# Norm factors and rotation of q and k moved to VectorE between the chunks of the delta rule, in a one-core decoder layer

## The chip, the cores and the metric

The kernel runs on one core of a Trainium2 chip. The metric is the device time of one execution in microseconds (us). The median of three executions before the change is 690.14 us.

## The reference, cut to what matters

One decoder layer over 512 positions of width 1024. A combined projection feeds two groups of heads: group A is a gated DeltaNet (a delta rule worked chunk by chunk, then a gated norm), group B is sliding-window attention over q and k that are first normalised per head and then rotated. The two outputs are joined, projected, gated and added to x. A mixture of experts (32 experts, two per position) follows. The change touches only the norm and rotation of q and k in group B:

```
q = rope(rms_norm(q.reshape(bsz, seq, SWA_Q_HEADS, HEAD_DIM), q_norm), positions)   # 8 heads of 64
k = rope(rms_norm(k.reshape(bsz, seq, SWA_KV_HEADS, HEAD_DIM), k_norm), positions)  # 2 heads of 64
# rope: x1, x2 = halves of a head; out = [x1*cos - x2*sin, x1*sin + x2*cos]
state = state * exp(g_last) + k_dec^T v_new     # delta rule: one step per chunk
```

## The kernel before, in words

The 512 positions lie as four blocks (`tb`, `n`) of 128 rows on the partitions. The mixer is written as five generators (`delta_rule`, `ropes`, `products`, `modulations`, `out_gdn`); `weave` (L56) hands their pieces over in the order of the numbers they yield. The framework then builds one queue per engine at compile time: a piece handed over earlier goes first where both could run, and a later one may go ahead where its inputs and buffers are there and the engine would be idle. On the chip each of the queues of VectorE, ScalarE and GpSimd runs in the order so built. `later(r, after)` (L252) adds an edge that orders two instructions in the same queue without a semaphore.

What stands around the change:

- `chunk(n)` (L706), key 67: the delta rule's step for 128 rows. TensorE forms products with the state (L713, L719), VectorE corrects X (L715, L716) and scales (L721), TensorE forms `p_vn` (L724) and `p_u` (L730), VectorE updates the state `Sbd` in two halves (L735, L736; a copy, L738, in chunk 0), TensorE forms the output `p_o` (L741), which L744 adds up. `join64` and `join32` (L665, L689) run between the chunks, with copies on VectorE (L685, L700).
- `products()` (L1110): the weight projections on TensorE. The last four (keys 67 to 92, `p_proj` at L263 to L265) give z; each is taken out of PSUM by ScalarE (L786, L787) and finished by VectorE (L788). At 92.5 comes `rope_turn(tb)` (L866): TensorE turns the rotated q and k (L872, L879), ScalarE writes them to `qrT` and `kg` (L873, L880). From 99 on comes `attend(tb, kv)` (L885): scores (L894, L898), maxima on VectorE (L901), exponentials on ScalarE, and so on.
- `ropes()` (L1166): `head_scale` (L838) squares on ScalarE and sums per head on VectorE (L845 for q, L846 for k), key 87.9; `rsqrt_n` (L182) makes the norm factors with 12 small VectorE instructions; `rope(tb)` (L848), key 92.2, multiplies and rotates. For q (128x512 per block) one product (L855) and six half-size instructions (L859 to L864, 128x256) run on VectorE; for k (128x128) the same seven (128x128 and 128x64) run on GpSimd.
- `out_gdn()` (L1193): `router_operands` (16 products `p_cst`, L1036), `gate_rows` (L980, products L986) for the gate g1, and the scaling of the output weights `wo` by g1 on VectorE (L1002), their split (L269, L270), and the output projection `p_wo`.
- Temporary tiles `hsq`, `rp`, `tz`, the angle tiles `ang` and `sin_w` and the attention's `pT` share one pool of three buffers, "w2" (`fill_tile`, L388).

After the mixer come the second half of the output projection, the routing, and the experts, whose weights (3 MB each) stream in from HBM as buffers come free.

Of the kernel before, what the change touches and what calls it, by code (L numbers as in the profile page):

```python
# [14 lines left out]
ALU = mybir.AluOpType  # L15
AX = mybir.AxisListType
# [3 lines left out]
P = 128  # L20
# [4 lines left out]
NH = 8  # L25
HD = 64
# [43 lines left out]
def hybrid_layer(ctx, tc, x, c, positions, w_ada, b_ada, norm_mix, w_in, conv_w, a_log, dt_bias,  # L70
# [4 lines left out]
    x = x[0]  # L75
# [3 lines left out]
    out = out[0]  # L79

    V, A, G, T = nc.vector, nc.scalar, nc.gpsimd, nc.tensor
# [14 lines left out]
    def psg(shape, name, dt=F32):  # L96
        return psG.tile(shape, dt, tag="psg", name=name)
# [18 lines left out]
    def sm(name, shape=(P, NT, NH), dt=F32):  # L116
        return small.tile(list(shape), dt, name=name)
# [19 lines left out]
    EN = {'V': V, 'G': G}  # L137
# [44 lines left out]
    def rsqrt_n(y, ss, scale, extra=None):  # L182

        t = mw.tile([P, NT * (NH + 2)], F32, tag="nt", name="newton_t")
        n = 1
        for d_ in y.shape[1:]:
            n *= d_
        t = t[:, :n]
        if len(y.shape) == 3:
            t = t.rearrange("p (a b) -> p a b", a=y.shape[1])  # L190
        V.tensor_scalar(ss, ss, scale, EPS, op0=ALU.mult, op1=ALU.add)
        yi = y.bitcast(I32)
        V.tensor_scalar(yi, ss.bitcast(I32), 1, None, op0=ALU.arith_shift_right)
        V.tensor_scalar(yi, yi, -1.0, float(0x5F3759DF), op0=ALU.mult, op1=ALU.add)
        for i in range(3):
            V.tensor_tensor(out=t, in0=ss, in1=y, op=ALU.mult)
            V.scalar_tensor_tensor(t, t, -0.5, y, op0=ALU.mult, op1=ALU.mult)
            V.scalar_tensor_tensor(y, t, 1.5, y, op0=ALU.add, op1=ALU.mult)
        if extra is not None:
            V.tensor_scalar(y, y, extra, None, op0=ALU.mult)  # L200
# [11 lines left out]
    def rms_rstd(src, name):  # L212

        sq = work.tile([P, D], F32, tag="w4", name=f"sq_{name}")
        st = work.tile([P, 1], F32, tag="st", name=f"st_{name}", bufs=4)
        A.activation(sq, src, AF.Square, accum_out=st)
        last_pow[0] = rsqrt_(st, st, 1.0 / D)
        return st
# [27 lines left out]
    for tb in range(NT):  # L246
        xx = xts[tb // 2][:, tb % 2]
        r = rms_rstd(xx, f"x{tb}")
# [3 lines left out]
    def later(r, after=None):  # L252

        tc.add_manual_dep(r.ins, after or hold, NOSYNC)
        return r
# [49 lines left out]
    for kb in range(KB):  # L305
# [17 lines left out]
        for b in range(4):  # L323
            n = slice(b * P, (b + 1) * P)
# [53 lines left out]
    for n in range(1, 4):  # L378
        for i in range(2):
            o = 32 * n + 8 * i  # L380
# [4 lines left out]
    def chain_tile(name, shape=(P, 512)):  # L385
        return mw.tile(list(shape), F32, tag="c2", name=name, bufs=3)

    def fill_tile(name, shape=(P, 512)):  # L388
        return mw.tile(list(shape), F32, tag="w2", name=name, bufs=3)
# [37 lines left out]
    def row_heads(t):  # L427
        return t.rearrange("p (h d) -> p h d", d=HD)

    def bc_n(t, n):  # L430
        return t[:, n, :, None].to_broadcast([P, NH, HD])
# [5 lines left out]
    eglP = sm("eglP", (P, NT, 4))  # L437
# [61 lines left out]
    big = {}  # L499
# [149 lines left out]
    def TT(m):  # L649
        return big[f"TT{m // 16}"][:, m % 16]  # L650
# [50 lines left out]


    Sbd = sm("Sbd", (P, 4, P))
    G.memset(Sbd, 0.0)

    def chunk(n):  # L706
        t = slice(n * P, (n + 1) * P)
        qT, knT, knat = big["qT"], big["knT"], big["knat"]
        X = big["vb"][:, n]
        if n:  # L710
            pk = psg([P, 512], f"p_ks{n}")
            for b in range(4):
                T.matmul(pk[:, b * P:(b + 1) * P], knT[:, b, t], Sbd[:, b], start=True, stop=True)  # L713
            ks = chain_tile(f"ks{n}")
            V.tensor_tensor(out=row_heads(ks), in0=row_heads(pk), in1=bc_n(bG, n), op=ALU.mult)  # L715
            V.tensor_tensor(out=X, in0=X, in1=ks, op=ALU.subtract)  # L716
            pq = psg([P, 512], f"p_qs{n}")
            for b in range(4):
                T.matmul(pq[:, b * P:(b + 1) * P], qT[:, b, t], Sbd[:, b], start=True, stop=True)  # L719
            qs = chain_tile(f"qs{n}")  # L720
            V.tensor_tensor(out=row_heads(qs), in0=row_heads(pq), in1=bc_n(eG, n), op=ALU.mult)  # L721
        pv = psg([P, 512], f"p_vn{n}")
        for h in range(NH):
            T.matmul(pv[:, h * HD:(h + 1) * HD], TT(n * NH + h), X[:, h * HD:(h + 1) * HD], start=True, stop=True)  # L724
        vn = chain_tile(f"vn{n}")
        A.activation(vn, pv, AF.Copy)
        if n < NT - 1:
            pu = psg([P, 4, P], f"p_u{n}")
            for b in range(4):
                T.matmul(pu[:, b], knat[:, n, b * P:(b + 1) * P], vn[:, b * P:(b + 1) * P], start=True, stop=True)  # L730
            for i in range(2):
                r = slice(64 * i, 64 * i + 64)
                sd = Sbd[r, :, r]
                if n:
                    V.tensor_tensor(out=sd, in0=sd, in1=eglP[r, n, :, None].to_broadcast([64, 4, HD]), op=ALU.mult)  # L735
                    V.tensor_tensor(out=sd, in0=sd, in1=pu[r, :, r], op=ALU.add)  # L736
                else:
                    V.tensor_copy(sd, pu[r, :, r])  # L738
        po = psg([P, 512], f"p_o{n}")
        for h in range(NH):  # L740
            T.matmul(po[:, h * HD:(h + 1) * HD], E[n][:, h], vn[:, h * HD:(h + 1) * HD],  # L741
                     start=True, stop=True)
        if n:
            V.tensor_tensor(out=X, in0=po, in1=qs, op=ALU.add)  # L744
        else:
            A.activation(X, po, AF.Copy)
# [91 lines left out]
    def head_scale(tb):  # L838

        q_, k_ = big["sq_n"][:, tb], big["skv"][:, tb, 0:P]  # L840
        sq = fill_tile(f"hsq{tb}")
        sk = mw.tile([P, P], F32, tag="hk", name=f"hsk{tb}", bufs=2)
        A.activation(sq, q_, AF.Square)
        A.activation(sk, k_, AF.Square)
        V.tensor_reduce(big["ssh"][:, tb, 0:NH], row_heads(sq), axis=AX.X, op=ALU.add)  # L845
        V.tensor_reduce(big["ssh"][:, tb, NH:], row_heads(sk), axis=AX.X, op=ALU.add)  # L846

    def rope(tb):  # L848

        rt, rs = big["rt"], big["rsh"]  # L850
        for src, nh, o, r0 in ((big["sq_n"][:, tb], NH, 0, 0), (big["skv"][:, tb, 0:P], 2, 4, NH)):
            s_ = row_heads(src)
            tmp = row_heads(fill_tile(f"rp{tb}{nh}")[:, :nh * HD])
            e_ = [EN[x] for x in 'VVVGGG'[3 * (nh == 2):]]
            EN['VG'[nh == 2]].tensor_tensor(  # L855
                out=s_, in0=s_, in1=rs[:, tb, r0:r0 + nh, None].to_broadcast([P, nh, HD]), op=ALU.mult)
            lo, hi, t_lo, t_hi = s_[:, :, :HH], s_[:, :, HH:], tmp[:, :, :HH], tmp[:, :, HH:]
            cl, sl, ch_, sh_ = (rt[:, o + i, tb, None, :].to_broadcast([P, nh, HH]) for i in (0, 1, 3, 2))
            e_[1].tensor_tensor(out=t_hi, in0=lo, in1=sh_, op=ALU.mult)  # L859
            e_[1].tensor_tensor(out=t_lo, in0=hi, in1=sl, op=ALU.mult)  # L860
            e_[0].tensor_tensor(out=lo, in0=lo, in1=cl, op=ALU.mult)
            e_[0].tensor_tensor(out=hi, in0=hi, in1=ch_, op=ALU.mult)
            e_[2].tensor_tensor(out=lo, in0=lo, in1=t_lo, op=ALU.subtract)
            e_[2].tensor_tensor(out=hi, in0=hi, in1=t_hi, op=ALU.add)  # L864

    def rope_turn(tb):  # L866

# [176 lines left out]
    def delta_rule():  # L1044
# [49 lines left out]
        for n in range(NT):  # L1094
            yield 67
            chunk(n)
            if n + 1 < NT:
                join64(n + 1)
            if n + 2 < NT:
                join32(n + 2)  # L1100
# [63 lines left out]
        slots.done("qrT", "sq_n", "sr")  # L1164

    def ropes():  # L1166
        yield 87.9
        big["ssh"], big["rsh"] = sm("ssh", (P, NT, NR)), sm("rsh", (P, NT, NR))
        for tb in range(NT):
            head_scale(tb)  # L1170
        rsqrt_n(big["rsh"], big["ssh"], 1.0 / HD)
        for tb in range(NT):
            yield 92.2 + 0. * tb
            rope(tb)

    def modulations():
        seq = [(r, kb) for r in (1, 2) for kb in range(KB)]
# [15 lines left out]
    def out_gdn():  # L1193
# [16 lines left out]
        slots.done("kg")  # L1210

    weave(delta_rule(), ropes(), products(), modulations(), out_gdn())
    sh2e, A2e, g2c = mod["sh2e"], mod["A2e"], mod["g2"]

# [262 lines left out]
    def at_lanes(lane8):  # L1477
        return V.tensor_tensor(out=so_t, in0=lane8[:, :, None].to_broadcast([P, 8, P]),
                               in1=laneb[:, None, :].to_broadcast([P, 8, P]), op=ALU.is_equal)
# [53 lines left out]
    after = at_lanes(l8).ins.name  # L1533
    keep_table(add_up(NS, "s", idle), 0, NS)
    for u in range(2):
# [20 lines left out]
                    in1=ident[0:NE, None, 0:NE].to_broadcast([NE, 2, NE]), op=ALU.mult)  # L1556
# [12 lines left out]
    ps, after = table(of_expert(sD, NSTAT, NE, "d"), NS, NU - NS, "d")  # L1569
# [209 lines left out]
    for k, u in enumerate(run):  # L1779
# [50 lines left out]
        if k >= NS and prepare:  # L1830
            V = Behind(nc.vector, g_.made)
            if next(prepare, 0) == 0:
                prepare = None
            V = nc.vector
# [56 lines left out]
```

## Time and profile before

| | us |
|---|---|
| median of three executions | 690.14 (689.63 to 705.21) |
| the profiled execution: its own time | 690.03 |
| the profiled execution: span, first to last instruction | 688.0 |
| TensorE busy in the span | 621.2 (90%) |
| VectorE / ScalarE / GpSimd busy | 387.2 / 243.7 / 182.2 |

The profiled execution's own time is 2.0 us longer than its span and 0.1 us below the median. Times in the rows below are us from the start of the span. PE is TensorE, PEld its weight loads, DVE VectorE, ACT ScalarE, POOL GpSimd. A timeline row has start, duration (for merged instructions from the first start to the last end), engine, line, operation, output and inputs, count, and in brackets the idle time before it and what ended it.

### The profile page before, as it was taken

The numbers are of one execution on the slowest core, as the hardware profiler recorded it, in microseconds if no ns is written. First come the engines' busy times: TensorE is split into PE (matmuls) and PEld (weight loads), VectorE is DVE, ScalarE is ACT, GpSimd is POOL, SyncE is SP. The second block draws the span as 40 slices with busy tenths as digits, with TensorE's granted clock in tenths as the row PEclk, the third lists the DMA queues.
The fourth block names the chain that finished last, engine by engine and source line by source line (L and its number), as shares of the span: only waits on it lengthen the run. The fifth ranks groups of instructions, "written<-read, shape, count | busy, mean of one in ns | idle before, by whom it ended". The sixth has DMA issues, their size and how long they took to land.

```text
span 688.0 us, 10766 instructions
## 1 busy us (share of the span) xinstructions
PE 621.2 (90%) x3907; PEld 378.7 (55%) x3908; DVE 387.2 (56%) x808; ACT 243.7 (35%) x546; POOL 182.2 (26%) x259
## 2 busy tenths in 40 slices
PE   6899799988888999988879998899999999999984
PEld 2576554646567978875447887334343334444521
DVE  3343986698999325688887348311342434444724
ACT  3235554232334442328772243413213232222200
POOL 2501315162263386063452002101001121111100
PEclk9799999997999999999989999999999999999998
DMA  8992374174310300251028849599999999999973
GB/s 256 293 318 65 122 279 164 62 250 162 123 61 23 102 2 12 90 216 62 1 64 302 335 156 354 203 399 416 412 414 403 411 410 406 408 408 410 408 296 123
DMA packets 62805, 161.78 MB, mean 235 GB/s; under 512 B 7175, under 2 KB 32931, under 8 KB 56608
## 3 DMA queue, kind: packets, MB, share of 16 engines
q1 hardware_dynamic: 57216, 148.52, 58.3%
q0 software_dynamic: 3952, 6.81, 2.9%
q10 hardware_dynamic: 1584, 5.77, 2.1%
q8 instruction: 31, 0.51, 0.3%
q14 instruction: 22, 0.18, 0.1%
HBM read 158.72 MB, written 8.39 MB: 243 GB/s over the span
## 4 chain that ended last, share of the span: by engine, by line
PE 45%; DMA 27%; DVE 20%; POOL 3%; issue 2%; ACT 2%; SPq 1%; POOLq 0%; ACTq 0%; DVEq 0%
DMA w_p<-in_w_up_dram 15%; DMA w_p<-in_w_down_dram 6%; PE p_gu L1600 5%; PE p_y L1636 3%; DMA w_p<-in_w_gate_dram 3%; DVE prod L643 3%; PE p_proj L265 3%; PE p_proj L263 3%; PE p_proj L264 3%; PE p_wo L264 2%; PE p_wo L265 2%; PE p_wo L263 2%; DVE cv L397 2%; DVE R L645 2%; PE p_ada L284 1%
## 5 line engine op out<-in xcount | busy, mean ns | idle before, releaser
L1600 PE MATMUL p_gu<-w_p,xT 128*32 128x512 f32 (+2 forms) x560 | 95.9, 594 | 0.0
L270 POOL TENSOR_TENSOR wH<-w,wH 128x512 fp32r<-128x512 f32 x36 | 52.4, 1472 | 125.9 <-ACT wH L269 112.8
L1600 PEld LDWEIGHTS p_gu<-w_p,xT 128*32 128x32 f32 (+2 forms) x560 | 32.0, 123 | 61.4 <-issue 55.8
L1519 POOL DMA_INDIRECT gb<-xn_d,ids x16 | 16.2, 1014 | 160.4 <-PE p_x L1587 146.4
L1636 PE MATMUL p_y<-w_p,hT 128*32 128x512 f32 (+2 forms) x280 | 51.3, 597 | 3.7 <-DVE hT L1624 2.6
L1609 DVE TENSOR_TENSOR hid<-hid,p_gu 128x256 f32<-128x256 f32 x16 | 6.7, 421 | 82.6 <-ACT hid L1608 82.6
L1608 ACT ACTIVATE hid<-p_gu 128x256 f32<-128x256 f32 x16 | 6.1, 384 | 126.8 <-PE p_gu L1600 126.8
L1593 ACT ACTIVATE xT<-p_x,sh2e,A2e 128x128 f32<-128x128 f32 x128 | 46.3, 467 | 12.1 <-PE p_x L1587 11.3
L1638 DVE SCALAR_TENSOR_TENSOR y<-p_y,wts,rsl 128x512 f32<-128x512 f32 x32 | 24.0, 749 | 41.5 <-PE p_y L1636 41.5
L265 PE MATMUL p_proj<-hH,wH 128*128 128x512 f32 x96 | 40.8, 425 | 0.0
L263 PE MATMUL p_proj<-hH,wH 128*128 128x512 f32 x96 | 40.5, 422 | 0.0
L264 PE MATMUL p_proj<-hL,wH 128*128 128x512 f32 x96 | 40.0, 417 | 0.0
L1656 PE MATMUL p_add<-yHL,to 128*128 128x512 f32 x128 | 35.5, 417 | 2.9 <-DVE xr L1661 1.9
L1656 PEld LDWEIGHTS p_add<-yHL,to 128*128 128x128 f32 x128 | 21.5, 188 | 19.7 <-DVE xr L1661 8.0
L1636 PEld LDWEIGHTS p_y<-w_p,hT 128*32 128x32 f32 (+2 forms) x280 | 14.8, 122 | 31.0 <-issue 24.4
L1661 DVE TENSOR_TENSOR xr<-xr,p_add 128x512 f32<-128x512 f32 x40 | 26.8, 686 | 6.9 <-PE p_add L1656 6.9
L263 PE MATMUL p_nat<-wH,hH 128*128 128x256 f32 x96 | 28.0, 291 | 0.0
L643 DVE TENSOR_TENSOR prod<-R 128x1 f32<-128x1 f32 (+30 forms) x31 | 27.2, 877 | 0.7
L265 PE MATMUL p_nat<-wH,hL 128*128 128x256 f32 x96 | 27.5, 286 | 0.0
L264 PE MATMUL p_nat<-wH,hH 128*128 128x256 f32 x96 | 27.5, 286 | 0.0
L263 PE MATMUL p_wo<-woH,mH 128*128 128x512 f32 x64 | 25.9, 404 | 0.0
L264 PE MATMUL p_wo<-woL,mH 128*128 128x512 f32 x64 | 25.7, 402 | 0.0
(523 smaller groups left out, 1362.2 us busy)
## 6 DMA issues: line engine op xcount, KB each, us to landing
w_p<-in_w_gate_dram SPq DMA_DIRECT2D x52, 512.0 KB
w_p<-in_w_up_dram SPq DMA_DIRECT2D x52, 512.0 KB
w_p<-in_w_down_dram SPq DMA_DIRECT2D x26, 1024.0 KB
ada<-in_w_ada_dram SPq DMA_DIRECT2D x16, 1024.0 KB
w<-in_w_in_dram SPq DMA_DIRECT2D x9, 1024.0 KB
ada<-in_w_ada_dram SPq DMA_DIRECT2D x12, 512.0 KB
w<-in_w_gate_dram SPq DMA_DIRECT2D x12, 512.0 KB
w<-in_w_up_dram SPq DMA_DIRECT2D x12, 512.0 KB
```

What stands on the lines that cost most here:

```text
L263: T.matmul(ps, aH, bH, start=first, stop=False)
L264: T.matmul(ps, aH, bL, start=False, stop=False)
L265: T.matmul(ps, aL, bH, start=False, stop=last)
L270: eng.tensor_tensor(out=lo, in0=src, in1=hi.bitcast(F32), op=ALU.subtract)
L643: V.tensor_tensor(out=pp, in0=Ti[:, :i, :i].rearrange("p j k -> p k j"), in1=Ms[:, :i, i][:, None, :].to_broadcast([P, i, i]), op=ALU.mult)
L1519: nc.gpsimd.indirect_dma_start(out=buf, out_offset=None, in_=xn_d[:, :], in_offset=bass.IndirectOffsetOnAxis(ap=ap, axis=0), bounds_check= ...
L1593: A.activation(self.xT[:, kb], pt[:, i], AF.Identity, bias=sh2e[:, kb:kb + 1], scale=A2e[:, kb:kb + 1])
L1600: self.last = T.matmul(self.ph[r], self.xT[:, kb, r], w[1 + kb // 4][:, :, kb % 4], start=(kb == 0), stop=(kb == KB - 1), tile_position=(0 ...
L1636: self.last = T.matmul(py[o:o + n], self.hT[:, i, o:o + n], w[3][:, i, cs], start=(i == 0), stop=(i == 1), tile_position=(0, o))
L1638: self.made = V.scalar_tensor_tensor(y[:, cs], py, self.w_ap, g2[:, cs], op0=ALU.mult, op1=ALU.mult).ins.name
L1656: t = T.matmul(ps, g_.to[:, tb * P:(tb + 1) * P], g_.yHL[:, i, cs], start=(2 * j + i == 0), stop=(2 * j + i == n - 1))
L1661: return V.tensor_tensor(out=x1(tb)[:, cs], in0=x1(tb)[:, cs], in1=ps, op=ALU.add).ins.name
```

## The change

The per-head sums of `head_scale` are ordered behind chunk 0's state copy, `rope(tb)` behind the sum that ends chunk 1's state update (L736; blocks 0 and 1), behind the product in chunk 2's (L735; block 2) and behind its sum (L736; block 3). The stream's keys go from 87.9 and 92.2 to 71 and 71.1 to 71.4. The k rotation moves from GpSimd to VectorE and comes before that of q.

```diff
+    state = {}
@@ def chunk(n):
-                    V.tensor_tensor(out=sd, in0=sd, in1=eglP[r, n, :, None].to_broadcast([64, 4, HD]), op=ALU.mult)
-                    V.tensor_tensor(out=sd, in0=sd, in1=pu[r, :, r], op=ALU.add)
+                    state[n, 0] = V.tensor_tensor(out=sd, in0=sd, in1=eglP[r, n, :, None].to_broadcast([64, 4, HD]),
+                                                  op=ALU.mult).ins.name
+                    state[n, 1] = V.tensor_tensor(out=sd, in0=sd, in1=pu[r, :, r], op=ALU.add).ins.name
                 else:
-                    V.tensor_copy(sd, pu[r, :, r])
+                    state[n, 1] = V.tensor_copy(sd, pu[r, :, r]).ins.name
@@ def head_scale(tb):
-        V.tensor_reduce(big["ssh"][:, tb, 0:NH], row_heads(sq), axis=AX.X, op=ALU.add)
-        V.tensor_reduce(big["ssh"][:, tb, NH:], row_heads(sk), axis=AX.X, op=ALU.add)
-
-    def rope(tb):
+        later(V.tensor_reduce(big["ssh"][:, tb, 0:NH], row_heads(sq), axis=AX.X, op=ALU.add), state[0, 1])
+        later(V.tensor_reduce(big["ssh"][:, tb, NH:], row_heads(sk), axis=AX.X, op=ALU.add), state[0, 1])
+
+    def rope(tb, after):
 
         rt, rs = big["rt"], big["rsh"]
-        for src, nh, o, r0 in ((big["sq_n"][:, tb], NH, 0, 0), (big["skv"][:, tb, 0:P], 2, 4, NH)):
+
+        def tt(out, a, b_, op):
+            later(V.tensor_tensor(out=out, in0=a, in1=b_, op=op), after)
+
+        for src, nh, o, r0 in ((big["skv"][:, tb, 0:P], 2, 4, NH), (big["sq_n"][:, tb], NH, 0, 0)):
...
-            EN['VG'[nh == 2]].tensor_tensor(
-                out=s_, in0=s_, in1=rs[:, tb, r0:r0 + nh, None].to_broadcast([P, nh, HD]), op=ALU.mult)
+            tt(s_, s_, rs[:, tb, r0:r0 + nh, None].to_broadcast([P, nh, HD]), ALU.mult)
...
-            e_[1].tensor_tensor(out=t_hi, in0=lo, in1=sh_, op=ALU.mult)
...
+            tt(t_hi, lo, sh_, ALU.mult)
+            tt(t_lo, hi, sl, ALU.mult)
+            tt(lo, lo, cl, ALU.mult)
+            tt(hi, hi, ch_, ALU.mult)
+            tt(lo, lo, t_lo, ALU.subtract)
+            tt(hi, hi, t_hi, ALU.add)
@@ def ropes():
-        yield 87.9
+        yield 71
...
-            yield 92.2 + 0. * tb
-            rope(tb)
+            yield 71.1 + .1 * tb
+            rope(tb, state[(1, 1, 2, 2)[tb], (1, 1, 0, 1)[tb]])
```

In `state[n, 0]` and `state[n, 1]` the loop over the two halves of `Sbd` leaves the names of the second half's product and sum.

## Rows read from the trace of the kernel before

**Rows 1.** The page, the chain that ended last: its shares by engine.
```profile
PE 45%; DMA 27%; DVE 20%; POOL 3%; issue 2%; ACT 2%; SPq 1%; POOLq 0%; ACTq 0%; DVEq 0%
```
**Rows 2.** Busy time by stretch; the first line names the columns.
```profile
core 0: us, PE busy (x) PEld busy (x) DVE busy (x) ACT busy (x) POOL busy (x), PEclk, DMA share, GB/s
250.00:268.30 18.30, 18.24 (x219) 15.95 (x218) 7.74 (x12) 6.67 (x14) 15.68 (x28) 1.00 0.01 2
268.30:294.40 26.10, 26.02 (x284) 22.27 (x284) 14.94 (x36) 7.44 (x15) 3.63 (x6) 1.00 0.30 98
294.40:301.60 7.20, 7.20 (x34) 5.91 (x33) 5.12 (x10) 1.09 (x2) 4.00 (x8) 1.00 0.52 171
301.60:354.80 53.20, 42.85 (x233) 25.86 (x232) 46.39 (x113) 37.32 (x113) 29.18 (x35) 0.90 0.19 71
...
301.60:418.00 116.40, 103.44 (x555) 74.20 (x554) 82.24 (x192) 59.71 (x157) 39.49 (x66) 0.96 0.45 164
...
440.00:669.00 229.00, 219.63 (x1210) 91.52 (x1206) 87.98 (x152) 61.47 (x158) 28.95 (x29) 1.00 1.01 402
```
**Rows 3.** The chain in order of time, 295 to 313: start, duration, piece.
```profile
295.00 2.56 DVE sq_n L855 x4
...
311.57 0.47 POOL sr L864
312.06 0.42 ACT kd L876
```
**Rows 4.** Timeline of PE, 301 to 317.
```profile
301.32 0.39 PE L265 MATMUL p_proj<-hH,wH 128*128 128x512 f32 x1
301.55 1.87 PE L1036 MATMUL p_cst<-rsl,sh 128*128 128x36 f32 x16
...
304.54 0.66 PE L872 MATMUL p_qrT<-ident,sq_n 128*128 128x128 f32 x4 [0.25 <-DVE sq_n L864]
...
307.76 0.49 PE L898 MATMUL p_s<-kg,qrT 64*128 64x128 f32 x4 [2.34 <-ACT kg L880]
...
314.36 2.05 PE L986 MATMUL p_gate<-ident,g 128*128 128x128 f32 x16 [0.47 <-ACT qrT L873]
```
**Rows 5.** Timeline of DVE, 253 to 318.
```profile
253.26 0.86 DVE L738 COPY Sbd<-p_u 64x256 f32<-64x256 f32 x2 [3.38 <-PE p_u L730]
...
263.83 2.30 DVE L735 TENSOR_TENSOR Sbd<-Sbd,eglP 64x256 f32<-64x256 f32 x2
267.36 0.87 DVE L736 TENSOR_TENSOR Sbd<-Sbd,p_u 64x256 f32<-64x256 f32 x2 [1.24 <-PE p_u L730]
...
294.40 0.69 DVE L744 TENSOR_TENSOR vb<-p_o,qs 128x512 f32<-128x512 f32 x1 [0.65 <-PE p_o L741]
...
303.61 0.41 DVE L863 TENSOR_TENSOR sq_n<-sq_n,rp 128x256 f32<-128x256 f32 x1
...
304.41 0.54 DVE L859 TENSOR_TENSOR rp<-sq_n,sr 128x256 f32<-128x256 f32 x1
...
312.67 1.07 DVE L901 TENSOR_REDUCE s<-p_s 128x2 f32<-128x256 f32 x3
...
317.08 1.22 DVE L1002 TENSOR_TENSOR wo<-wo,kg 128x1024 f32<-128x1024 f32 x1 [1.93 <-ACT kg L989]
```
**Rows 6.** Timeline of POOL, 262 to 305.
```profile
262.71 3.13 POOL L270 TENSOR_TENSOR wH<-w,wH 128x512 fp32r<-128x512 f32 x2
...
293.74 1.47 POOL L855 TENSOR_TENSOR sr<-sr,rsh 128x128 f32<-128x128 f32 x4 [21.40 <-DVE oss L765]
...
304.17 0.49 POOL L860 TENSOR_TENSOR rp<-sr 128x64 f32<-128x64 f32 x1
```
**Rows 7.** DVE groups by line and form, 250 to 302: count, busy us, mean ns.
```profile
L845 DVE TENSOR_REDUCE ssh<-hsq 128x8 f32<-128x512 f32 x4 | 2.5, 678 | 0.3 <-ACT hsq L843 0.3
...
L196 DVE TENSOR_TENSOR newton_t<-ssh,rsh 128x40 f32<-128x40 f32 x3 | 0.6, 197 | 0.1
```

More of the change, by code (lines that the diff above doesn't have):

```diff
@@ L844, in head_scale @@
         A.activation(sk, k_, AF.Square)
-        V.tensor_reduce(big["ssh"][:, tb, 0:NH], row_heads(sq), axis=AX.X, op=ALU.add)
-        V.tensor_reduce(big["ssh"][:, tb, NH:], row_heads(sk), axis=AX.X, op=ALU.add)
-    def rope(tb):
+        later(V.tensor_reduce(big["ssh"][:, tb, 0:NH], row_heads(sq), axis=AX.X, op=ALU.add), state[0, 1])
+        later(V.tensor_reduce(big["ssh"][:, tb, NH:], row_heads(sk), axis=AX.X, op=ALU.add), state[0, 1])
+    def rope(tb, after):
         rt, rs = big["rt"], big["rsh"]
-        for src, nh, o, r0 in ((big["sq_n"][:, tb], NH, 0, 0), (big["skv"][:, tb, 0:P], 2, 4, NH)):
+        def tt(out, a, b_, op):
+            later(V.tensor_tensor(out=out, in0=a, in1=b_, op=op), after)
+        for src, nh, o, r0 in ((big["skv"][:, tb, 0:P], 2, 4, NH), (big["sq_n"][:, tb], NH, 0, 0)):
             s_ = row_heads(src)
             tmp = row_heads(fill_tile(f"rp{tb}{nh}")[:, :nh * HD])
-            e_ = [EN[x] for x in 'VVVGGG'[3 * (nh == 2):]]
-            EN['VG'[nh == 2]].tensor_tensor(
-                out=s_, in0=s_, in1=rs[:, tb, r0:r0 + nh, None].to_broadcast([P, nh, HD]), op=ALU.mult)
+            tt(s_, s_, rs[:, tb, r0:r0 + nh, None].to_broadcast([P, nh, HD]), ALU.mult)
             lo, hi, t_lo, t_hi = s_[:, :, :HH], s_[:, :, HH:], tmp[:, :, :HH], tmp[:, :, HH:]
             cl, sl, ch_, sh_ = (rt[:, o + i, tb, None, :].to_broadcast([P, nh, HH]) for i in (0, 1, 3, 2))
-            e_[1].tensor_tensor(out=t_hi, in0=lo, in1=sh_, op=ALU.mult)
[L860 to L864, printed above, removed]
+            tt(t_hi, lo, sh_, ALU.mult)
[4 more added lines that the diff above has]
+            tt(hi, hi, t_hi, ALU.add)
     def rope_turn(tb):
```

## The prediction

> **What bounds the kernel now.** I read the chain of waits first, then busy time by stretch, then the timelines of the engines around the change. The chain is TensorE for 45%, DMA for 27% and VectorE for 20% [rows 1], so the limit differs by stage. Four stages matter.
>
> From 250 to 301.6 us TensorE is full: 18.24 of 18.3, 26.02 of 26.1 and 7.20 of 7.20 us busy [rows 2], because the z projections fill the holes of the chunks. VectorE is not: 7.74 of 18.3, 14.94 of 26.1, 5.12 of 7.2. The last chunk's output is added at 294.40 [rows 5], the last projection product starts at 301.32 [rows 4].
>
> From 301.6 to about 313 the rotation is the bound. The chain goes through the scaling of q on VectorE at 295.00, then the k rotation on GpSimd until 312.04, then a copy on ScalarE [rows 3]. TensorE starts the turns at 304.54 and the scores at 307.76 after 2.34 us of waiting, but VectorE takes the first maxima only at 312.67, when its last rotation is through [rows 4, 5].
>
> From 312.67 to 354.8 attention, gated norm and the preparation of the output weights share VectorE, which is busy 46.39 of the 53.2 us from 301.6 [rows 2]. From 354.8 to 418 the output projection fills TensorE.
>
> From 440 to 669 the expert weights hold the DMA engines (share 1.01, 402 GB/s) [rows 2]. That stage has fixed bytes. It starts when the routing has been computed and buffers are free, so an earlier mixer starts it, and ends it, earlier by as much.
>
> **The change part by part.** *Rotation of q.* Four products of 128x512 take 2.56 us together, 0.64 each [rows 3]. A 128x256 instruction takes 0.41 us where GpSimd is idle and 0.54 beside GpSimd's k rotation [rows 5]; they start some 0.07 us before the last one's end, so 0.34 or 0.46 apart. Between the chunks GpSimd is idle: from 272 on it stands 21.4 us before its first k product [rows 6]. So I take 0.34: 4 x (0.64 + 6 x 0.34) = 10.7 us. With 0.46 it is 13.6.
>
> A rule of the Trainium skill bears on that: "SBUF — State Buffer", section "SBUF: two separate sides", says that a VectorE instruction with two SBUF inputs and a GpSimd instruction that reads SBUF lock each other out for a whole instruction. The rows agree: beside GpSimd, VectorE falls from 0.41 to 0.54 us [rows 5, 6], and one of two 64x256 state products lasts until GpSimd's split is over, 2.30 us for the pair [rows 5, 6]. By the rule the rotation also ran at GpSimd's pace before, and the sum of 10.7 stands; without it the sum would be 13.6.
>
> *Rotation of k.* Seven instructions per block leave GpSimd and come to VectorE, where no 128x128 or 128x64 of this kind stands in these rows. The bounds are 0.197 us (128x40) [rows 7] and 0.41 (128x256) [rows 5]. 128x64 lies nearest to the lower, 128x128 between: 0.21 and 0.29, less the overlap of 0.07. 0.22 + 6 x 0.14 = 1.1, four blocks 4.2 us; ends 4 x 7 x 0.13 = 3.6 and 4 x 7 x 0.34 = 9.5.
>
> *Sums and norm factors.* Four sums for q of 0.678 us [rows 7], about 0.61 apart, four small ones for k, at most 0.34 each, and 12 instructions of some 0.2 [rows 7] move to the time behind chunk 0's copy, which ends at 254.1 [rows 5]. That is 2.4 + 1 + 2.8 = 6.2 us in the 10.6 us that VectorE stands idle in 250 to 268.3 [rows 2]. They cost nothing while that cover holds; if ScalarE's squares keep VectorE standing behind each of the four in turn, about 0.7 each, 3 us.
>
> *Does the rotation fit?* It may start at 268.2, where chunk 1's sum ends [rows 5]. From there to 301.6 VectorE has 33.3 us, of which 20.1 are used [rows 2]. Of these, 2.4 and 2.8 us of sums and factors go earlier, and 2.6 of scaling and 0.5 of rotation are counted anew. That leaves 11.8 of other work; with 10.7 + 4.2 it is 26.7, so 6.6 us stay free. With both upper ends, 13.6 + 9.5, it is 34.9, and 1.6 us would run over.
>
> *What it does to the chunks.* Each chunk has four places where TensorE waits for VectorE (two copies, the corrected X, the state). A rotation instruction already running delays each by at most 0.64 us, on average about 0.2; three chunks, twelve places: 2.4 us, at most 7.7. I cost it at nothing: after the chunks' last output at 294.4, projections still fill TensorE for 7.2 us [rows 2], and they can be taken earlier. Without that cover it is 2.4 us.
>
> *The z gates.* Their tiles come from the ring of three that the rotation's temporaries use, and now stand behind these in it. So the first two come only when chunk 2's update has let the third block's rotation go. Four PSUM banks hold all four projections meanwhile, so TensorE needn't stop. No DMA moves with the change; SP's queue holds none of it, and on GpSimd's queue nothing is passed but the 28 k instructions that leave it.
>
> *The gain.* The turns no longer wait. Before, from the first turn to the first score took 307.76 - 304.54 = 3.2 us [rows 4]. From the projections' end that gives scores at 304.8, done 0.5 later, and the first maxima at 305.3 instead of 312.67: 7.4 us. Second way: the gate g1 releases the weight scaling at 317.08 [rows 5]. In front of it on TensorE stand p_cst (1.87), four turns of about 1.04 (0.66 for q, the rest for k) and the gate itself (2.05), 8.1 us, so it ends at 309.7 instead of 316.4: 6.7 us. If the first scores (16 products, 2 us) and 1.5 us of masks and gated-norm turns go ahead too, 3.1 us. I take 7.0, between the first two ways, since the turns and the gate have the earlier keys. What is late next is VectorE in attention: 46.39 us less some 11 of rotation in that stage leaves 35.4 busy, and with the 6.8 idle the stage would last 42.2, 11 us shorter. So VectorE allows 7.
>
> The sum against the profiled execution: 690.0 - 7.0 = 683.0 us. Its own time is 0.1 below the median, so the forecast for a median is the same.
>
> **The rivals.** *Most of it is lost behind (687).* The output projection could start no earlier than the split weights, which go through VectorE, ScalarE and GpSimd between attention's steps, or scores go ahead of the gate. For it: the second way's lower result, 3.1 us; 690 - 3 = 687. Against: everything in that stage follows from the same start.
>
> *More is gained (679).* With GpSimd free and VectorE relieved, the stage shrinks by the 11 us that VectorE's account allows. For it: TensorE is idle 116.4 - 103.4 = 13.0 us between 301.6 and 418 and its mean granted clock is 0.96 [rows 2]. Against: most of that idle time lies in attention's chain, which stays. These 13 us also bound the gain: over 2% (13.8 us; about what a measurement of this kernel can tell from no change) would need the clock as well.
>
> *The rotation holds up the chunks (699).* VectorE's queue is in order. If a rotation or sum put ahead of chunk 1 to 3's copies waits for its input, the chunk waits too, and with it TensorE. The place is the sums behind 254.1 and the first rotation behind 268.2: their squares need ring buffers that the angles hold until GpSimd is through with them and turns to its next split, 262.71 [rows 6]. It decides from 14.2 us of waiting, the 7.2 of filler and the 7.0 of gain; a wait until the chunks' end, 295 less 272, 23 us, gives 690 + 23 - 14 = 699. Against: the factors are due by 265 and the first rotation needs them at 268. The Trainium skill, "Perfetto Trace Analysis", section "Per-engine timelines", also has ACT, DVE and GPSIMD as strict FIFO; the 21.4 us for which GpSimd stood before its k product [rows 6] agree.
>
> *It doesn't do what it says (689.5).* If the built queue leaves the rotation at the end after all, only the lock falls away: 13.6 - 10.7 = 2.9 us, less 4.2 of k work on VectorE and what GpSimd no longer holds up, near nothing.
>
> **How the numbers follow.** Forecast 683: 0.52. Lost behind: 0.22. More gained: 0.14. Held up: 0.07. Not done: 0.05. The range leaves out the far part of the held-up case and a few of the largest gains: 677 to 691. It contains the 3.1 and the 11 us of gain, and a loss of 2.4 in the chunks on top of the smaller. Faster by over 2% (below 676.3) 0.05, from the far end of the larger gain; slower by over 2% (above 703.9) 0.03, from a held-up time longer than 28 us; within 2% 0.92.
>
> **What would show it.** Right: rotation instructions on VectorE between 268 and 300 at 0.41 us, none on GpSimd; the projections' last product within 2 us of 301.3; the first maxima at about 305; the first weight scaling at about 310; the output projection's end and the saturated DMA stage 7 us earlier at 402 GB/s. Wrong: TensorE idle between 250 and 301; rotation after 302; the first maxima early but the output projection not; a gain up to 418 that the DMA stage gives back.

## The result, and the profile after

| | before | after |
|---|---|---|
| median (executions), us | 689.88 (4) | 710.36 (4) |
| lowest to highest | 687.98 to 705.21 | 707.92 to 712.71 |
| profiled execution: its own time / span | 690.03 / 688.0 | 712.71 / 711.0 |

The ratio after to before is 1.0282, 95% interval 1.0241 to 1.0323: slower by some 20 us, where 7 us less was forecast. Executions of one kernel differ by up to 17 us here, the longer ones at a lower mean granted clock, so a ratio with its 95% interval stands beside each median below; rows are of profiled executions.

The way to read it is by marks. Between the same five events of both traces stand these times (us). The marks are ScalarE's copy `vn` of chunk 0, the last projection product, VectorE's first scaling of the output weights (`wo`), the last row of logits products (L1281, now L1285), and the end of the span. Lines from about 740 on have moved by 2, from about 860 on by 4.

| stretch | before | after | difference |
|---|---|---|---|
| start to chunk 0's `vn` | 251.39 | 265.70 | +14.31 |
| to the last projection product | 49.93 | 51.45 | +1.52 |
| to the first weight scaling | 15.76 | 10.79 | -4.97 |
| to the last row of logits | 99.80 | 111.98 | +12.18 |
| to the end | 271.12 | 271.08 | -0.04 |

So two losses of 14.3 and 12.2 us stand against a gain of 5.0 less 1.5. The expert stage only starts later.

*The first loss.* Busy time by stretch of the changed kernel; the columns are those of [rows 2]. In the first row TensorE does nothing for ten microseconds and comes back at half clock (1.2 GHz); before, it was busy 18.24 of 18.3 us there [rows 2].

```profile
250.00:260.00 10.00, 0.00 (x0) 0.00 (x0) 0.00 (x0) 0.35 (x1) 9.84 (x21) 0.56 0.00 0
260.00:270.00 10.00, 9.31 (x89) 8.73 (x90) 1.56 (x4) 2.90 (x7) 2.52 (x7) 0.59 0.00 0
```

What TensorE waited for is one row of its timeline, and what that waited for is in ScalarE's:

```profile
247.40 0.69 PE L673 MATMUL p_y<-TT,Mn 32*32 32x32 f32 x32
260.60 0.65 PE L681 MATMUL p_z<-y,Mn 32*32 32x32 f32 x3 [11.61 <-ACT y L676]
```

```profile
245.68 0.59 ACT L696 ACTIVATE yy<-p_yy 64x512 f32<-64x512 f32 x1
259.65 0.63 ACT L845 ACTIVATE hsq<-sq_n 128x512 f32<-128x512 f32 x1 [13.38 <-POOL ang L831]
260.19 0.76 ACT L676 ACTIVATE y<-p_y 32x256 f32<-32x256 f32 x2
```

The product `p_y` of the second join was there at 248.1. Its copy `y` (L676) needs nothing else, but in ScalarE's queue the square of block 1 (L845) stands ahead of it, and that needs a ring buffer which the angle tile holds until GpSimd's L831. In the kernel before, the squares came at 281 and later, and the same copy had only its product to wait for:

```profile
247.91 0.77 ACT L676 ACTIVATE y<-p_y 32x256 f32<-32x256 f32 x2 [2.24 <-PE p_y L673]
```

Read the idle time in the brackets first, then the row behind it: that is the one that pays. The Trainium skill, "Perfetto Trace Analysis", section "Per-engine timelines", has ACT, DVE and GPSIMD as strict FIFO; the row agrees, with 13.38 us.

*The gain.* VectorE's timeline shows what was forecast: rotation between the chunks, at 0.41 us for 128x256. Chunk 1's pair of state products takes 0.86 us, 2.30 before [rows 5]; that is not the change's doing, since GpSimd's split of weights, which held it up, now falls at 273.29, ahead of it. The first maxima come 5.5 us behind the last projection product (317.15), before 11.35.

```profile
280.48 0.86 DVE L736 TENSOR_TENSOR Sbd<-Sbd,eglP 64x256 f32<-64x256 f32 x2
...
289.68 0.41 DVE L855 TENSOR_TENSOR sq_n<-sq_n,sr 128x256 f32<-128x256 f32 x1
290.01 0.75 DVE L855 TENSOR_TENSOR sq_n<-sq_n,rp 128x256 f32<-128x256 f32 x2
290.69 0.34 DVE L855 TENSOR_TENSOR rp<-sr 128x64 f32<-128x64 f32 x2
...
322.69 0.75 DVE L905 TENSOR_REDUCE s<-p_s 128x2 f32<-128x256 f32 x2 [2.54 <-PE p_s L902]
```

*The second loss.* Attention, by stretch, first of the kernel before, then of the changed one. The three rows of each run from about the last projection product to the first scaling, from there to the first product of the output projection, and from there to the last logits.

```profile
301.60:317.10 15.50, 11.45 (x84) 9.23 (x82) 13.53 (x35) 8.41 (x26) 9.64 (x22) 0.89 0.42 160
317.10:354.80 37.70, 31.40 (x150) 16.62 (x150) 32.86 (x79) 28.91 (x89) 19.54 (x13) 0.91 0.10 35
354.80:416.90 62.10, 59.49 (x316) 47.25 (x314) 35.40 (x77) 22.39 (x46) 9.77 (x31) 1.00 0.67 241
```

```profile
317.50:327.90 10.40, 10.29 (x85) 8.17 (x83) 4.07 (x15) 7.97 (x24) 0.89 (x2) 1.00 0.69 256
327.90:371.80 43.90, 39.57 (x131) 20.08 (x130) 28.93 (x70) 25.60 (x77) 16.68 (x10) 0.61 0.07 24
371.80:439.90 68.10, 63.97 (x332) 50.18 (x332) 36.27 (x85) 25.52 (x55) 13.17 (x33) 0.97 0.60 220
```

The middle row is 6.2 us longer although VectorE has less to do in it; its clock is 0.61. Over the last two rows TensorE stands no longer than before, 8.5 us in place of 8.9; it is busy for 103.5 us in place of 90.9. So the 12 us are products that take longer, not waits. In finer stretches of the changed kernel the clock falls behind a stand of TensorE and then stays low, with TensorE full:

```profile
333.00:336.40 3.40, 0.90 (x4) 0.44 (x4) 3.40 (x4) 1.86 (x7) 2.35 (x2) 1.00 0.00 0
336.40:345.00 8.60, 7.88 (x26) 4.11 (x26) 6.04 (x18) 4.98 (x13) 4.66 (x2) 0.50 0.01 2
345.00:360.00 15.00, 15.00 (x42) 7.36 (x41) 7.51 (x18) 7.30 (x24) 4.05 (x4) 0.50 0.00 0
360.00:370.00 10.00, 9.74 (x30) 5.25 (x28) 6.53 (x18) 5.43 (x12) 4.20 (x3) 0.50 0.21 73
```

What made it stand: TensorE's row, VectorE's, and GpSimd's, all of the changed kernel.

```profile
336.43 1.06 PE L925 MATMUL p_pT<-ident,p 128*128 128x128 f32 x4 [2.53 <-DVE p L920]
```

```profile
331.82 2.13 DVE L911 TENSOR_TENSOR s<-s,sink 128x4 f32<-128x4 f32 x1
333.87 1.21 DVE L1006 TENSOR_TENSOR wo<-wo,kg 128x1024 f32<-128x1024 f32 x1
335.00 1.68 DVE L920 TENSOR_SCALAR p<-p,s 128x128 f32<-128x128 f32 x3
```

```profile
331.58 2.35 POOL L270 TENSOR_TENSOR woL<-wo,woH 128x1024 fp32r<-128x1024 f32 x1 [13.10 <-ACT woH L269]
334.78 1.42 POOL L777 TENSOR_TENSOR mL<-og,mH 128x512 fp32r<-128x512 f32 x1 [0.85 <-ACT mH L776]
```

A sum of 128x4 lasts 2.13 us beside GpSimd's split, which began 0.24 us before it; a weight scaling stands behind it; and the scaled `p` for which TensorE waits is late. Such a meeting is not new. In the kernel before, small instructions of VectorE were held up beside each of the four splits, here one of 128x4 (VectorE, then GpSimd):

```profile
329.88 2.32 DVE L909 TENSOR_TENSOR s<-s,s 128x4 f32<-128x4 f32 x1
```

```profile
329.57 2.61 POOL L270 TENSOR_TENSOR woL<-wo,woH 128x1024 fp32r<-128x1024 f32 x1 [0.33 <-ACT woH L269]
```

There TensorE's longest stand from the first scaling to 354.8 was 1.53 us, and the half clock lasted some 7 us. New is the stand of 2.53 us and the 34 us at 0.50 behind it.

### The profile page after: what moved, and what is told of

It is laid out like the page before. It is cut to its first block, busy times and chain, and to the rows that moved or that the text cites. A ratio compares the mean times of both kernels' runs of the same rounds, so it can differ in the third digit from the quotient of the medians.

```text
span 711.0 us, 10772 instructions
## 1 busy us (share of the span) xinstructions
PE 635.1 (89%) x3908; PEld 386.6 (54%) x3908; DVE 385.0 (54%) x836; ACT 244.0 (34%) x546; POOL 169.5 (24%) x231
## 4 chain that ended last, share of the span: by engine, by line
PE 49%; DMA 26%; DVE 16%; POOL 3%; ACT 2%; issue 2%; SPq 1%; POOLq 0%; ACTq 0%
DMA w_p<-in_w_up_dram 15%; DMA w_p<-in_w_down_dram 6%; PE p_gu L1604 5%; PE p_y L1640 3%; PE p_proj L265 3%; PE p_proj L263 3%; DMA w_p<-in_w_gate_dram 3%; DVE prod L643 3%; PE p_proj L264 3%; PE p_s L902 2%; PE p_wo L264 2%; PE p_wo L265 2%; PE p_wo L263 2%; DVE cv L397 2%; DVE R L645 2%
```

## The experiments

Each row of the table gives the same five stretches for one kernel, and for the fourth, attention from the first scaling to the last logits, the mean granted clock and the time for which TensorE stands idle. `w4` is the work buffer pair that lies unused between the inverse and attention. e6, e10 and e11 have products added in attention.

| kernel | to `vn` | to last projection | to scaling | to logits | its clock | its idle time | to end |
|---|---|---|---|---|---|---|---|
| e2_act_pin | 249.27 | 57.08 | 10.80 | 107.29 | 0.87 | 8.9 | 271.26 |
| e3_only_sums | 265.59 | 52.00 | 16.86 | 101.18 | 0.95 | 9.3 | 274.27 |
| e4_w4_ring | 260.44 | 51.06 | 10.80 | 111.69 | 0.83 | 8.5 | 271.31 |
| e5_act_pin2 | 252.05 | 51.15 | 10.83 | 113.28 | 0.83 | 9.6 | 273.49 |
| e6_w4_busy | 258.19 | 51.10 | 10.16 | 109.02 | 0.95 | 11.5 | 273.03 |
| e7_w4_kg | 262.19 | 57.01 | 10.80 | 109.99 | 0.84 | 8.2 | 273.11 |
| e9_pin2_wov | 249.23 | 51.15 | 10.82 | 98.94 | 0.98 | 10.0 | 275.56 |
| e10_pin2_busy_wov | 248.83 | 51.12 | 10.66 | 101.56 | 1.00 | 6.3 | 272.93 |
| e11_before_busy | 249.43 | 49.95 | 15.75 | 110.40 | 0.95 | 10.3 | 272.77 |
| e12_before_wov | 250.92 | 49.92 | 15.78 | 97.83 | 0.97 | 7.4 | 273.65 |
| e13_after_wov | 263.16 | 51.91 | 10.79 | 94.55 | 1.00 | 8.6 | 273.39 |

The kernel before has 99.80 us at 0.97 with 8.9 us idle, the changed one 111.98 at 0.83 with 8.5. In the kernels without added products the idle time hardly differs (7.4 to 10.0 us), and the stretch goes with the clock: 107 to 113 us at 0.83 to 0.87, 94.6 to 101.2 at 0.95 to 1.00. The column to `vn` differs by some 3 us between kernels without a hole, and the last one by 4.5, so differences of that size in them are not read.

**The sums alone.** The kernel before, with key 71 for squares, sums and factors, and the sums pinned as in the changed kernel; the rotation stays late.

```diff
-        yield 87.9
+        yield 71
...
-        V.tensor_reduce(big["ssh"][:, tb, 0:NH], row_heads(sq), ...)
+        later(V.tensor_reduce(big["ssh"][:, tb, 0:NH], row_heads(sq), ...), state[0, 1])
...
```

> The kernel before, with only the squares and sums put where the changed kernel has them; the factors and the rotation run after that as the shares of GpSimd and VectorE were, without being pinned behind the chunks. Theory (the loss is made by the early squares alone, on ScalarE): the wait for the ring is there again, 12 to 14 us in front of hsq of block 1, and the time is 702 to 712. Rival (the loss is the rotation's, on VectorE between the chunks): the time is within 5 us of the kernel before, 685 to 695.

Measured 707.35 us (ratio 1.0223, 1.0150 to 1.0296). ScalarE's timeline has the same row:

```profile
259.54 0.63 ACT L844 ACTIVATE hsq<-sq_n 128x512 f32<-128x512 f32 x1 [13.39 <-POOL ang L830]
```

The rotation did not move between the chunks, and the first loss is all there. It belongs to the squares on ScalarE. The second loss is not there: attention takes 101.18 us at 0.95, with the split on GpSimd.

**The squares moved one step back.** In the changed kernel, with its buffers:

```diff
-            A.activation(X, po, AF.Copy)
+            state["o"] = A.activation(X, po, AF.Copy).ins.name
...
-        A.activation(sq, q_, AF.Square)
-        A.activation(sk, k_, AF.Square)
+        later(A.activation(sq, q_, AF.Square), state["o"])
+        later(A.activation(sk, k_, AF.Square), state["o"])
```

> The changed kernel, with its buffers as they are, but the eight squares on ScalarE ordered behind chunk 0's output copy, which comes after the angles are through on GpSimd. Theory (it is the place in ScalarE's queue that costs, not the ring as such): the wait of 13.38 us goes, since the ring buffer is free by the time the squares come to the head of the queue; time as in the variant with buffers of their own, within 3 us: 683 to 694. Rival (the rotation on VectorE costs the chunks, or the ring costs in any place because the squares, now late, delay the factors and with them the rotation): the last projection product at 301 to 303, but the first row maxima no sooner than in the kernel before (312.67), time 688 or more and the rows of the chunks longer than before.

The variant with buffers of their own that this names (e1_own_ring) could not be run; that much SBUF is not left. Measured 701.96 us (1.0167, 1.0096 to 1.0237): better than the changed kernel, short of the 683 to 694 that was expected; the last projection product comes at 306.35, which neither theory had. The `vn` mark is back (249.27), but the wait has only moved: ScalarE's timeline shows squares that still wait, now ahead of the third join's `y`, for which TensorE stood 4.17 us at 262.09 and came back at half clock.

```profile
257.32 0.63 ACT L845 ACTIVATE hsq<-sq_n 128x512 f32<-128x512 f32 x1 [2.49 <-POOL ang L831]
...
260.22 0.63 ACT L845 ACTIVATE hsq<-sq_n 128x512 f32<-128x512 f32 x1 [2.07 <-POOL sr L836]
...
261.68 0.76 ACT L676 ACTIVATE y<-p_y 32x256 f32<-32x256 f32 x2
```

**The squares moved two steps back**, behind the last copy of the third join:

```diff
-        A.activation(M_[32:64, n * NH:(n + 1) * NH, 64:96], pz[32:64], AF.Copy)
+        state["j", n] = A.activation(M_[32:64, n * NH:(n + 1) * NH, 64:96], pz[32:64], AF.Copy).ins.name
...
-        A.activation(sq, q_, AF.Square)
+        later(A.activation(sq, q_, AF.Square), state["j", 2])
... (the same for k)
```

> The changed kernel with its buffers as they are, but the eight squares on ScalarE ordered behind the last copy of the third join (join32 of chunk 2), one step later than in the run before, where the squares still stood ahead of that join's y (4.17 us of TensorE's waiting there). Theory (what counts is what stands behind the waiting square in ScalarE's queue): nothing that TensorE needs at once stands behind it, TensorE is busy throughout 245 to 265, the last projection product at 299 to 305, time 683 to 697 as for the variant with other buffers. Rival (any place costs, since late squares make the factors and the rotation late): the last projection product at 299 to 305 but first row maxima over 8 us after it.

Measured 701.14 us (1.0140, 1.0043 to 1.0236). The theory on ScalarE's queue holds: no square waits, TensorE is busy 14.82 of 15 us from 250 to 265, the last projection product comes at 303.20. The time does not follow, and lies above the range given. The loss is the attention stretch, 113.28 us, again mostly at half clock:

```profile
314.00:367.90 53.90, 45.10 (x171) 24.91 (x167) 41.32 (x93) 33.10 (x101) 19.63 (x13) 0.68 0.06 20
```

**Other buffers for the squares.**

```diff
-        sq = fill_tile(f"hsq{tb}")
+        if tb % 2 == 0:
+            state["sq"] = work.tile([P, 2, 512], F32, tag="w4", name=f"hsq{tb}")
+        sq = state["sq"][:, tb % 2]
```

> The changed kernel, with the squares of q in the two work buffers w4, two blocks to each, which lie unused between the inverse and attention, in place of the ring that the angles hold; nothing is pinned anew. Theory (ScalarE's wait for the ring makes the loss): no square waits for GpSimd, TensorE is busy throughout 245 to 265, the last projection product comes at 299 to 304 and the first row maxima 5 to 7 us after it (kernel before: 11.35). The time is then 683 to 686 if TensorE's clock stays up in attention, and 690 to 697 if attention runs some 27 us at half clock as in the two runs with early factors so far. Rival (the rotation on VectorE, not the ring, holds up the chunks): the last projection product at 308 or later and a time of 700 or more.

Measured 708.92 us (1.0299, 1.0203 to 1.0395). Neither theory had this: the time and the last projection product, 311.50, are as the rival had them, but not by the rotation. No square waits, yet the hole is there: with other buffers the built queues differ too. GpSimd has the angles ahead of the weight split, and ScalarE's next split waits for its buffer, again ahead of `y`. ScalarE, then GpSimd, of this kernel:

```profile
253.87 1.15 ACT L269 ACTIVATE wH<-w 128x512 fp32r<-128x512 f32 x2 [11.93 <-POOL wH L270]
254.92 0.76 ACT L676 ACTIVATE y<-p_y 32x256 f32<-32x256 f32 x2
```

```profile
249.74 0.46 POOL L796 TENSOR_TENSOR ang<-ang 128x128 f32<-128x128 f32 x1
250.16 0.31 POOL L828 TENSOR_SCALAR sin_w<-sin_w 128x128 f32<-128x128 f32 x1
250.43 0.54 POOL L795 TENSOR_SCALAR ang<-ang 128x128 f32<-128x128 f32 x1
250.93 1.27 POOL L270 TENSOR_TENSOR wH<-w,wH 128x512 fp32r<-128x512 f32 x1
```

So the ring is one way into the hole; the common part is an instruction on ScalarE that waits for GpSimd's chain of angles, with the join's copy behind it.

**The k rotation back on GpSimd**, on the w4 variant (`G.tensor_tensor` for `nh == 2`, unpinned):

> The variant with the squares in w4, with the k rotation back on GpSimd, unpinned; the q rotation stays on VectorE between the chunks. It tells what the engine of the k rotation is worth by itself. Theory (GpSimd is idle there and only the place in time matters): within 3 us of the variant with k on VectorE. Rival (VectorE's time between the chunks is short, or the lock between VectorE and GpSimd costs): over 3 us away from it, shorter in the first case, longer in the second.

Measured 717.06 us (1.0393, 1.0261 to 1.0525), 8 us over its base, or 6 without its longest execution (729.78). VectorE's products beside it are longer (1.00 us for two of 128x256 at 292.42, 0.76 at 298.39, where GpSimd is done), as [rows 5] had it, and ScalarE's copy of the rotated k now waits for GpSimd ahead of the next join's `y`:

```profile
290.01 0.42 ACT L885 ACTIVATE kd<-sr 128x256 f32<-128x256 f32 x1 [4.68 <-POOL sr L858]
```

From `vn` to the last projection product it takes 57.0 us in place of 51.1. On this base VectorE is the better engine for k; the two ways in which GpSimd costs are not told apart.

**Products to hold the clock up in attention.** Their results are overwritten, nothing of the computation is left out.

```diff
...
+            for _ in range(12 if b == 0 else 0):
+                last = later(T.matmul(pt[:, 0:2], upper.bitcast(BF16)[:, 0:P], upper.bitcast(BF16), start=True, stop=True),
+                             last).ins.name
```

> The variant with the squares in w4, plus 12 products of 128x256 in bf16, whose result is overwritten, ahead of the first turn of p in each of attention's eight steps, pinned behind the step's scores. Theory (the gain of the early rotation is given back in attention because TensorE stands a few us beside VectorE's and GpSimd's lock, its granted clock falls to 0.50 and then every product takes twice as long): the granted clock stays above 0.9 from 320 to 355 and the time is 5 to 9 us below that of the variant without these products, if that one has the half clock. Rival (attention's chain through VectorE sets the pace and TensorE at half clock merely fills its own idle time): the clock stays up but the time is the same within 2 us, or longer by up to the 10 us of added products.

> The variant with the squares pinned behind the third join (TensorE busy throughout the delta rule, last projection product at 303.2), plus the 12 overwritten bf16 products ahead of the first turn of p in each step of attention. In the variant without them TensorE stood 2.62 us for the scaled p at 325.5, its granted clock fell to 0.50 and stayed near there until 367, and the output projection began at 367.89 (kernel before: 354.80), although the maxima had begun 2.3 us earlier. Theory (the half clock is what gives the gain back): with the clock above 0.9 from 320 to 360 the output projection begins at 350 to 356 and the time is 683 to 690. Rival (attention's chain through VectorE and GpSimd makes the stage long, TensorE's clock only goes with it): the clock stays up, yet the output projection begins after 360 and the time is 696 or more. If the clock falls all the same, neither is tested.

> Control: the kernel before, with the same overwritten products in attention. Its profile shows the half clock for 344 to 350 alone. Theory (the products work through the clock alone): 0 to 3 us below the kernel before, since only some 6 us run at half clock there. Rival (the products help or hurt by reordering attention, whatever the clock): over 4 us away from the kernel before in either direction.

Measured 708.07 us (1.0288, 1.0177 to 1.0399) for e6_w4_busy, 702.92 (1.0139, 1.0022 to 1.0257) for e8_pin2_busy, 700.20 (1.0115, 0.9994 to 1.0235) for e11_before_busy. None helped. In e6 TensorE still waited 4.07 us for `p`, and its clock fell after that (0.51 from 331.6 to 342). In the control e11 the attention stretch grew by 10.6 us, with 13.1 us of such products in it and a half clock of its own (0.53 from 320 to 331). The profiled execution of e8 is its longest, 712.87 us, and its `vn` mark lies 9 us behind that of e5, so no row of it is read. The condition of the theory, a clock above 0.9 throughout, was not met (0.85 from 320 to 355 in e6). But e6 had 0.95 over the whole stretch where its base e4 had 0.83, and without its 13.1 us of added products the stretch is 96 us in place of 111.69. By this estimate the clock was worth about what the products cost.

**The split on VectorE.**

```diff
-            split(high[:, b], low[:, b], t[:, b], EN['GGVV'[i]])
+            split(high[:, b], low[:, b], t[:, b], EN['VVVV'[i]])
```

> The variant with the squares pinned behind the third join, with the low parts of the first four scaled weight pieces (woL) taken on VectorE in place of GpSimd. Theory (VectorE's small instructions last until GpSimd's split is over, 2.35 us for a 128x4 sum, 2.42 for three scalings of p, and that gap is what lets TensorE stand and its clock fall): VectorE has 4 x 1.2 us more to do, loses no instruction to the split, TensorE has no wait over 2 us between 312 and 340 and the time is 5 us or more below the 701 of that variant. Rival (VectorE is full in attention with or without the lock): the time is the same or up to 5 us longer.

> The changed kernel with nothing but woL on VectorE; the square's wait of 13.4 us in ScalarE's queue stays. Theory (the loss is two terms, 14.3 us in front of chunk 0's vn and 12.2 us in attention, less 3.5 of gain): the hole at 250 to 260 is as before, the attention stage is 11 to 14 us shorter and the time is 696 to 701. Rival (both come from one cause, the hole shifting what follows): the attention stage stays at 110 or more and the time over 706.

> Control: the kernel before, with woL on VectorE as in the fastest variant so far (686.8). It tells what of that variant is the early rotation and what the split alone. From the first weight scaling to the last logits the profiled runs took 99.8 us in the kernel before, 112.0 in the changed one, 113.3 with the squares pinned, 98.9 with the squares pinned and woL on VectorE. Theory (the collision with GpSimd's split costs 12 to 13 us only in the built order that the early rotation brings): this kernel stays within 3 us of the kernel before, 687 to 694, and the early rotation is then worth 0 to 5 us in the fastest variant. Rival (the split on GpSimd costs in every order): the time falls here too, to 683 or less, and the early rotation is worth nothing.

> Both edits together on the variant with the squares pinned behind the third join: overwritten products ahead of the turns of p, and woL on VectorE. If clock and lock each cost, this is the fastest: clock above 0.9 from 312 to 360, output projection from 350, time 680 to 686, under both kernels. If it is no better than the better of the two single edits, they had the same cause.

On the variant with pinned squares (e9): 686.78 us, ratio to the kernel before 0.9946 (0.9901 to 0.9992), 14.4 us below the same kernel with the split on GpSimd (701.14); TensorE's longest wait from 312 to 340 is 1.05 us. On the changed kernel as it is (e13): a median of 702.30 us, ratio 1.0167 (1.0071 to 1.0264), from two executions of 695.57 and 697.16 at a mean granted clock of 0.958 and two of 707.44 and 709.41 at 0.939 and 0.936. The shorter two lie at the lower end of the theory's 696 to 701, the median just above it. Of the longer two there is no trace; they are about as long as the changed kernel, and whether attention fell to half clock in them is not known. The profiled execution, 695.57, has the hole still (`vn` at 263.16) and an attention stretch of 94.55 us in place of 111.98. Attention by stretch, e13 first, then e9:

```profile
325.90:361.00 35.10, 28.18 (x166) 15.02 (x165) 30.91 (x82) 29.31 (x89) 10.15 (x9) 1.00 0.09 31
361.00:420.40 59.40, 57.70 (x299) 45.91 (x297) 34.30 (x76) 21.61 (x42) 8.72 (x30) 1.00 0.69 254
```

```profile
311.20:347.80 36.60, 27.34 (x153) 14.89 (x150) 30.70 (x82) 28.09 (x86) 11.27 (x9) 1.00 0.08 30
347.80:410.10 62.30, 61.55 (x315) 48.27 (x313) 36.22 (x81) 23.49 (x46) 8.88 (x30) 0.97 0.65 241
```

VectorE's timeline of e13 shows the same sum as above, and the split that VectorE now does itself:

```profile
329.73 0.13 DVE L911 TENSOR_TENSOR s<-s,sink 128x4 f32<-128x4 f32 x1
329.78 1.22 DVE L270 TENSOR_TENSOR woL<-wo,woH 128x1024 fp32r<-128x1024 f32 x1
330.92 0.68 DVE L920 TENSOR_SCALAR p<-p,s 128x128 f32<-128x128 f32 x3
```

2.13 us have become 0.13, three scalings of `p` 0.68 instead of 1.68, and the clock stays at 1.00 (2.4 GHz). The Trainium skill, "SBUF — State Buffer", section "SBUF: two separate sides", says that the pair of ports which VectorE and GpSimd share is held for a whole instruction while the other is blocked; the pair 2.13 and 0.13 agrees. The Trainium skill, "Perfetto Trace Analysis", section "Optimizing Scalar/DVE Operations", warns that moving work between these two engines might not help for that reason; here the way back to VectorE is worth 14 us in e9 and some 2 in attention without the early rotation (e12, below).

The control (e12) without the early rotation: 690.72 us, ratio 0.9957 (0.9912 to 1.0001). In the kernel before the split cost little, 99.80 to 97.83 us in attention, although VectorE was held up there too. So the split is dear only in the order that the early rotation brings, where a long half clock follows. A stand of TensorE alone does not bring that: e9 has one of 2.72 us before 347.42 and e12 one of 3.30 before 350.75, and their clocks are 0.98 and 0.97. The early rotation, freed of both losses, differs from its control by less than the intervals: 0.9946 to 0.9957. By the marks e9 reaches the last logits 4.3 us sooner than e12 (1.7 of it already at `vn`, ahead of the rotation), and gives back 1.9 of that afterwards. Adding the overwritten products (e10) gave 689.96 (0.9963, 0.9913 to 1.0013), no better than the single edit: its attention is at 1.00 throughout, but e9 had 0.98 without them.

## Why the prediction was wrong

**The step that failed first** is "Sums and norm factors ... They cost nothing while that cover holds". It counted VectorE's idle time, and for ScalarE's squares only what VectorE would lose. It did not ask what is queued behind a square on ScalarE. That is the join's copy `y`; it cost 14.3 us. The rival "The rotation holds up the chunks" had the cause, squares that need buffers held by the angles, but on VectorE's queue and from 254.1 on; it happened on ScalarE's, at 246.3. Its argument against, that the factors are due only by 265, was true of VectorE and beside the point on ScalarE. Its 699 us is near what the changed kernel would give with that loss alone, 690 + 14.3 - 3.5 = 701, but by chance: its sum was a wait of 23 us less 14 of filler and gain. Its chance of 0.07 was too small: the buffers and who holds them were in the text.

**The second** is "What is late next is VectorE in attention ... So VectorE allows 7". That took busy time for room, and counted nothing for a change of TensorE's clock. The relief of VectorE was real (32.86 us busy before the output projection, 28.93 after), and TensorE's idle time stayed the same; but TensorE's products took 12.6 us longer (90.9 to 103.5 us busy from the first scaling to the last logits), with the clock at 0.50 from 336.4 to 370. That price, 12.2 us, was in none of the cases. The lock had been weighed for the rotation alone. That the split on GpSimd starts this in the new order is shown by e9 against e5, and by the profiled execution of e13, where the stretch is 17.4 us shorter at 1.00. That it costs by the clock rests on the busy and idle times of the ten kernels without added products. No run held the clock up with the split on GpSimd and nothing else changed, and why it stayed down for 34 us is open.

**The gain** was mis-sized: 7.0 forecast, 3.45 measured (4.97 less 1.52), and 3.7 in e5 (4.93 less 1.22). The lowest of the three ways, 3.1 us, was the nearest: the first scores and masks do go ahead of the gate, which starts 6.90 us after the last projection product in place of 13.04. The scaling then stands in VectorE's queue for 1.2 us more (327.94, where its input was there at 326.78).

**The chunks**: "2.4 us, at most 7.7. I cost it at nothing". From chunk 0's `vn` to the last chunk's output product the time went from 41.05 to 43.42 us in e5, so 2.4 was right. The cover was not whole: 1.2 us come out at the last projection product in e5, and 1.5 in the changed kernel.

**Right were** the sizes of the instructions (0.41 us, 0.20 and 0.29 for k), the fit of the rotation between the chunks, the lock's end for the rotation, z gates that stop nothing, and the expert stage, which moved with its start (271.08 us to the end, 271.12 before; the other kernels have 271.3 to 275.6).

## What to carry to other kernels

When a step moves earlier, write down for every engine it uses which instruction will stand behind it in the queue, and what that step still waits for; an engine with much idle time is the easiest to overlook. A saved stretch changes the order in the next stage: look there for a new stand of TensorE and for its clock behind it, and compare busy time as well as idle time, since a lower clock shows in busy time alone. Measure by marks between events, not by the total: here three terms of 5, 12 and 14 us stood in one number.

## What the runs showed of the hardware

- At half clock TensorE stayed there with its queue full: from 345 to 360 it was busy 15.00 of 15.00 us at 0.50, and it was at 0.97 again only from 370 to 380, where it was busy 6.96 of 10 us. In the kernel before the half clock of attention ended after some 7 us (343 to 350). What ends it these runs do not tell.
- A VectorE instruction of 128x4 cost nearly as much as the GpSimd instruction beside it, 2.13 us to 2.35, and 0.13 alone.
- What such meetings cost the kernel does not follow from their number: the kernel before has one at each of its four splits, and taking the splits away shortened attention by 2 us there (e12) and by 14 to 17 us where a long half clock followed (e9 against e5, e13 against the changed kernel).
- The same built program takes 688.80 us at a mean granted clock of 0.963, 694.05 at 0.955 and 705.36 at 0.935, in one set of 17 executions of the kernel before: a hundredth of clock goes with some 6 us.
